# Differential score products over 64 rows each, in alternate halves of the array

## The chip, the cores and the metric

The kernel runs on one core of one Trainium2 chip. The metric is the time of one execution in microseconds of device time, the median of several runs; smaller is better.

## The reference

One decoder layer, in float32: 2048 positions, width 1024. A norm, a projection to queries, keys and values, two groups of attention heads beside each other, an output projection, a residual sum, and an MLP of width 4096 with a squared ReLU. The change touches the differential heads alone. There are four; each has two maps of 64 dimensions, whose softmaxes are subtracted:

```python
def diff_attn_block(q1, q2, k1, k2, v, lam, slopes, q0):
    def probs(q, k):
        s = jnp.einsum('bhqd,bhkd->bhqk', q, k).astype(jnp.float32) * scale + bias
        s = jnp.where(causal, s, -jnp.inf)
        return jax.nn.softmax(s, axis=-1)

    a = probs(q1, k1) - lam * probs(q2, k2)
    return jnp.einsum('bhqk,bhkd->bhqd', a.astype(v.dtype), v)
```

Eight stick-breaking heads of 64 dimensions stand beside them, with a product over later positions in place of the softmax.

## The kernel before

**Precision.** TensorE works on a rounded 4-byte type (`F32R`). To keep the result close to float32, each operand is split into a high part and a low part (what the rounding dropped), and a product is a sum of partial products: high by high, high by low, low by high. Dense products (`product`) have three partial products for each 128 rows of contraction.

**Scores.** A map has 64 dimensions, half of the array's 128 rows. The kernel before fills the other half with the key's low part: `load_k` puts the high part of both maps' keys into partitions 0 to 63 and the low part into 64 to 127 (dimension `t` of the scratch tensor `d_qk`, beside map `m`, row `r`, column `c`). The query must then stand in both halves, so `load_q` loads it twice, once into each; `j` chooses its high or its low part. One map's scores of 128 queries against up to 512 keys are two products over 128 rows: the high query against both parts of the key, and the low query against both. On the diagonal, columns left of `c0` are not computed, so that products of 512, 384, 256 and 128 columns occur. After the two products, VectorE adds the position bias on the way out of PSUM and takes the extreme value (`tensor_tensor_reduce`), and ScalarE takes the exponent.

**Loops.** `emit_diff` is called for each head and each block of 512 queries; in it run two groups `g` of 256 queries, over the key blocks `cc` before them, over two tiles `i2` of 128 queries, and over the two maps `m`. That gives 320 score tiles. Later steps of it weigh the maps, transpose the result on TensorE, and multiply by the values. `emit_sb` has 320 score tiles of its own.

**Order.** Nothing runs in the order in which it is written. Calls are recorded by `Plan.add` as units: on TensorE, successive products into the same tile are one unit, up to `LIMIT` (8). There are three streams, `dense` (projections, output, MLP), `diff` and `sb`. `Plan.order` then plays the program through with a duration for each unit (`Plan.duration`), and whenever an engine is free it takes the best unit that is ready and whose tiles find room. On TensorE attention units go first, and dense units fill what is left. `place` finds the room: PSUM has eight banks, and `caps` allows two of them to hold scores (`s`), of both kinds of heads together. `used` counts the banks held, `queue` keeps the tiles of one kind and stream in order. What comes out is a fixed list for each engine; on the chip an engine that waits holds up everything behind it in its list. All transfers are issued by one queue, SP's, in the planned order.

**Blocks.** The four blocks of 512 positions are worked in turn: projections of blocks 3 and 2, attention of 3 and 2 beside the projections of 1 and 0 and the first dense work after it, and so on; the MLPs of the last blocks stand alone at the end.

Of the kernel before, what the change touches and what calls it, by code (L numbers as in the profile page):

```python
# [20 lines left out]
F32R = mybir.dt.float32r  # L21
# [7 lines left out]
P = 128  # L29
# [3 lines left out]
HD = 64  # L33
HW = 256
# [72 lines left out]
class Plan:  # L107

    LIMIT = 8

    def __init__(self, homes):
        self.units, self.stream = [], "dense"
# [10 lines left out]
    def add(self, eng, fn, method, args, kw):  # L125
        views = [(k, v) for k, v in [*enumerate(args), *kw.items()] if isinstance(v, View)]
        outs = [v for k, v in views if k in ("out", "accum_out", 0)]
        ins = [v for k, v in views if k not in ("out", "accum_out", 0)]
        out = (outs or ins)[0]
        u = self.units[-1] if self.units else None  # L130
        if not (eng == "PE" and u and u.eng == "PE" and u.out is out.tile and len(u.calls) < self.LIMIT
                and u.stream == self.stream):
            u = Unit(len(self.units), eng, self.stream)
            u.out = out.tile
            self.units.append(u)
        u.calls.append((fn, args, kw))
        u.dur += self.duration(eng, method, kw, out, ins, u)
        for v in ins:
            for lo, hi, w in v.tile.writes:
                if lo < v.cols[1] and hi > v.cols[0]:  # L140
                    u.deps.add(w)
            v.tile.reads.append((*v.cols, u))
        for v in outs:
            for lst in (v.tile.writes, v.tile.reads):
                for lo, hi, w in lst:
                    if lo < v.cols[1] and hi > v.cols[0]:
                        u.deps.add(w)
                lst[:] = [x for x in lst if not (v.cols[0] <= x[0] and x[1] <= v.cols[1]) or x[2] is u and lst is v.tile.reads]
            v.tile.writes.append((*v.cols, u))
        if eng == "PE":  # L150

            u.deps.update(w for w in out.tile.units if w.eng == "PE")
        u.deps.discard(u)
        for v in outs + ins:
            if not v.tile.units or v.tile.units[-1] is not u:
                v.tile.units.append(u)
            if v.tile.home is not None and v.tile.units[0] is not u:
                u.deps.add(v.tile.units[0])

    def duration(self, eng, method, kw, out, ins, u):  # L160
        n = math.prod(out.shape[1:])
        small = [v for v in ins if math.prod(v.shape[1:]) * 4 > n]
        sb = [v for v in small if v.tile.home != "psum"]
        if eng == "PE":
            if kw.get("lhsT", kw.get("in_")).dtype == F32:
                return 0.112
            return max(0.058, n * 0.000442 + 0.001)
        if eng == "DVE":
            u.dual = len(sb) > 1
            u.psum = any(v.tile.home == "psum" for v in ins)  # L170
            if method == "tensor_tensor_scan":
                return 0.15 + n * 0.0022
            if method == "tensor_reduce":
                n = math.prod(ins[0].shape[1:])
            if method == "tensor_copy" and sb and n >= 256:
                u.dual = True
                return 0.43
            extra = 0.055 if isinstance(kw.get("scalar"), View) else 0.085 if "accum_out" in kw else 0.0
            return 0.15 + n / 960 + extra
        if eng == "ACT":  # L180
            u.psum = any(v.tile.home == "psum" for v in ins)
            extra = 0.09 if isinstance(kw.get("scale"), View) or isinstance(kw.get("bias"), View) else 0.0
            return 0.18 + (0.0 if u.psum else 0.03) + n / 1200 + extra + (0.19 if "accum_out" in kw else 0.0)
        if eng == "POOL":
            if method == "memset":
                return 0.2 + n / 1000
            if kw.get("op") == ALU.pow:
                return 1.65
            u.dual = True
            if method == "tensor_tensor":  # L190
                return 0.19 + n * (0.00216 if out.dtype == F32R else 0.00165)
            if method == "affine_select":
                return 0.3
            return 0.19 + n * 0.00085
        row = min([out.shape[-1]] + [v.shape[-1] for v in ins])
        u.bytes = math.prod(out.shape) * 4
        u.moves = u.bytes / {P: 265e3, HW: 300e3, BW: 335e3, D: 360e3}.get(row, 200e3)
        return 0.06


    def order(self, slots, phase_of, caps, log=None):
# [28 lines left out]
        queue = {}  # L230
# [19 lines left out]
        used = {}  # L250
# [44 lines left out]
        done, out = 0, []  # L295
# [7 lines left out]
        while done < len(units):  # L303
# [14 lines left out]
            while progress:  # L318
                progress = False
                for e in avail:  # L320
# [3 lines left out]
                    for u in waiting[e]:  # L324
                        if u.ready > now + 1e-9:
                            continue
                        k = self.key(u, now)
                        if best is not None and k >= best[0]:
                            continue
                        if u.stream == "dense" and u.i > dense[at_dense].i + self.AHEAD:  # L330
                            continue
                        spots, ok = [], True
                        for t in u.allocs:
                            if queue[u.stream, self.line(t)][-1] is not t:
                                ok = False
                                break
                            s = place(t, now)
                            if s is None:
                                ok = False
                                break  # L340
                            spots.append((t, s))
                            if len(u.allocs) > 1:
                                free[s[0]].remove(s[1])
                        if len(u.allocs) > 1:
                            for t, s in spots:
                                free[s[0]].append(s[1])
                        if ok:
                            best = k, u, spots
                    if best is None:
# [2 lines left out]
                    _, u, spots = best  # L352
# [9 lines left out]
                    start = now  # L362
                    if u.dual:
                        start = max(now, lock["POOL" if e == "DVE" else "DVE"])
# [33 lines left out]
                    for t in users.get(id(u), ()):  # L398
# [7 lines left out]
                        if not t.left:  # L406
                            kind, name = t.slot
# [43 lines left out]
def layer_kernel(ctx: ExitStack, tc: tile.TileContext, a: dict, out: bass.AP):  # L451
# [13 lines left out]
    plan = Plan(homes)  # L465
# [9 lines left out]
    def att(tag, shape, dtype=F32):  # L475
        return tile_view(tag, shape, dtype, tag)

    def dma(out, in_):

        f = [x.bitcast(F32) if x.dtype == F32R else x for x in (out, in_)]  # L480
        sp.dma_start(out=f[0], in_=f[1])

    def ps(tag):
        return tile_view("psum", [P, BW], F32, tag)
# [250 lines left out]
    def emit_diff(h, b):  # L735
        nch = NB - b

        def load_q(g):

            src = d_qk["dq", h, b][:, :, :, g * HW:(g + 1) * HW].rearrange("m t r c -> r m t c")  # L740
            qa = att("qa", [P, 2, 2, HW], F32R)
            for i in range(2):
                dma(qa[i * HD:(i + 1) * HD], src)
            return qa

        def load_k(c):
            ka = att("ka", [P, 2, BW], F32R)
            dma(ka, d_qk["dk", h, c].rearrange("m t r c -> (t r) m c"))
            return ka

        def load_v(c, kp):
# [5 lines left out]
        for g in range(NQ // 2):  # L757
# [3 lines left out]
            qa = load_q(g)  # L761
            for cc in range(nch):
                ka = load_k(b + cc)
                for i2 in range(2):
                    i = 2 * g + i2
                    c0 = i * P if cc == 0 else 0
                    for m in range(2):
                        s = ps("s")
                        qs = slice(i2 * P, (i2 + 1) * P)
                        for j in range(2):  # L770
                            pe.matmul(out=s[:, c0:], lhsT=qa[:, m, j, qs], rhs=ka[:, m, c0:], start=j == 0, stop=j == 1)

                        nm = negm[:, i2, m, cc:cc + 1]
                        t = att("e", [P, BW])
                        vec.tensor_tensor_reduce(out=t[:, c0:], in0=s[:, c0:], in1=bias[:, cc == 0, 0:BW - c0],
                                                 scale=-SLOPES[h], scalar=3e38, op0=ALU.add, op1=ALU.min, accum_out=nm)
                        act.activation(out=t[:, c0:], in_=t[:, c0:], func=ACTF.Exp, scale=-1.0, bias=nm,
                                       accum_out=l[:, i2, m, cc:cc + 1])
                        e[cc, i2, m] = t
                        yield  # L780
# [22 lines left out]
            for cc in range(nch):  # L803
                for i2 in range(2):
                    c0 = (2 * g + i2) * P if cc == 0 else 0
# [382 lines left out]
```

## Time and profile before

| | us |
|---|---|
| median of 3 runs (lowest, highest) | 2986.47 (2984.6, 2993.63) |
| the profiled execution | 2983.26 |
| its span, first to last instruction | 2981.5 |

The views used below are: the profile page (busy time of each engine and its share of the span); busy time by stretches; waits by engine; the chain of work that ended last; groups of instructions of one operation and shape (busy time, mean length of one, idle time of the engine just before them); and the timeline, in which neighbours of one kind are merged into one line with a count. All instructions go through one helper, so all have the line L446, and groups are told apart by tiles: `s<-ka,qa` are differential scores, `s<-ska,sq` those of the stick-breaking heads, `d` and `dn` dense products, `pt` transposes. PE is TensorE, PEld its weight loads, SPq the queue that issues transfers. Ends of matmuls in the trace are modelled, their starts are not.

### The profile page before, as it was taken

How to read it: one execution, taken by the hardware profiler on the slowest of the kernel's cores; microseconds unless marked ns; L12 is line 12 of the kernel's file. 1: busy time of each engine (PE TensorE's matmuls, PEld its weight loads, DVE VectorE, ACT ScalarE, POOL GpSimd, SP SyncE). 2: the span in 40 equal slices, each digit the busy share in tenths (PEclk: the TensorE clock that was granted, in tenths of full speed). 3: DMA queues.
4: the chain of work that ended last, by engine and by line, in shares of the span. 5: the costliest groups of instructions: out<-in, count | busy, mean ns of one | idle time of the engine just before them, and what ended most of it. 6: DMA issues, size and time to landing. Idle time of an engine off the chain costs nothing. (4 is left out here: it accounts for less than half of the span.)

```text
span 2981.5 us, 42384 instructions
## 1 busy us (share of the span) xinstructions
PE 2897.2 (97%) x14928; PEld 2438.1 (82%) x14928; DVE 1776.1 (60%) x3193; ACT 1146.2 (38%) x2390; POOL 1096.3 (37%) x1589
## 2 busy tenths in 40 slices
PE   8999999999999999999999999999999999999997
PEld 6889889888877887888788888888888888888886
DVE  5243477777788878786687788888543333421112
ACT  4232245555555655554354555555220110211001
POOL 3221266544776876866444344444100000000000
PEclk9999999999999999999999999999999999999998
DMA  7776988766976777877856565555874556635551
GB/s 260 254 239 204 280 255 256 216 219 210 312 247 228 249 257 241 268 255 266 313 197 204 186 198 190 189 190 172 315 270 176 205 174 243 253 132 214 204 190 65
DMA packets 304164, 670.51 MB, mean 225 GB/s; under 512 B 26960, under 2 KB 121424, under 8 KB 303952
## 3 DMA queue, kind: packets, MB, share of 16 engines
q1 hardware_dynamic: 303952, 667.80, 66.5%
q8 instruction: 119, 1.95, 0.3%
q14 instruction: 93, 0.76, 0.1%
HBM read 491.53 MB, written 176.16 MB: 224 GB/s over the span
## 5 line engine op out<-in xcount | busy, mean ns | idle before, releaser
L446 PE MATMUL d<-b,w 128*128 128x512 f32 x5376 | 1297.9, 395 | 15.0 <-ACT b L446 12.2
L446 PEld LDWEIGHTS d<-b,w 128*128 128x128 f32 x5376 | 1004.8, 189 | 233.5 <-ACT b L446 12.6
L446 PE MATMUL dn<-y,w 128*128 128x512 f32 x3072 | 748.5, 395 | 1.4 <-DVE b L446 1.1
L446 PEld LDWEIGHTS dn<-y,w 128*128 128x128 f32 x3072 | 573.2, 188 | 129.1 <-DVE b L446 1.3
L446 DVE TENSOR_TENSOR b<-b,dn 128x512 f32<-128x512 f32 x416 | 284.1, 684 | 300.9 <-PE dn L446 297.2
L446 POOL TENSOR_TENSOR w<-x,w 128x256 fp32r<-128x256 f32 x384 | 327.4, 874 | 256.3 <-ACT w L446 203.8
L446 POOL TENSOR_TENSOR set<-ser 128x512 f32<-128x512 f32 (+3 forms) x320 | 315.1, 987 | 114.8 <-DVE ser L446 100.2
L446 POOL TENSOR_TENSOR rrx<-rvx,mhalf 128x4 f32<-128x4 f32 x12 | 12.1, 1008 | 861.1 <-DVE rvx L446 861.1
L446 ACT ACTIVATE d<-d 128x512 f32<-128x512 f32 x128 | 74.8, 585 | 604.9 <-DVE d L446 604.6
L446 DVE TENSOR_TENSOR_SCAN ser<-set,left 128x512 f32<-128x512 f32 x192 | 274.7, 1435 | 9.6 <-POOL set L446 6.9
L446 DVE SCALAR_TENSOR_TENSOR d<-d,b 128x512 f32<-128x512 f32 x128 | 89.0, 698 | 303.1 <-PE d L446 294.3
L446 ACT ACTIVATE e<-e,negm 128x512 f32<-128x512 f32 (+3 forms) x320 | 209.9, 656 | 130.9 <-DVE negm L446 127.0
L446 ACT ACTIVATE hb<-pt 128x512 fp32r<-128x512 f32 (+1 forms) x320 | 164.4, 532 | 184.3 <-PE pt L446 108.6
L446 POOL TENSOR_SCALAR set<-set 128x512 f32<-128x512 f32 (+1 forms) x160 | 111.7, 698 | 315.9 <-ACT set L446 311.5
L446 DVE TENSOR_TENSOR hb<-pt,hb 128x512 fp32r<-128x512 f32 (+1 forms) x320 | 187.6, 602 | 48.5 <-ACT hb L446 46.7
L446 ACT ACTIVATE set<-s 128x512 f32<-128x512 f32 (+1 forms) x320 | 165.2, 533 | 131.1 <-PE s L446 122.3
L446 PE MATMUL d<-w,b 128*128 128x256 f32 x1536 | 201.7, 286 | 5.3 <-DMA w<-d_w_v 2.4
L446 DVE CUSTOM_DVE_ANT_0 e<-s,bias 128x512 f32<-128x512 f32 (+3 forms) x320 | 191.6, 599 | 24.8 <-PE s L446 24.5
L446 PEld LDWEIGHTS d<-w,b 128*128 128x128 f32 x1536 | 192.2, 191 | 10.8 <-DVE y L446 5.3
L446 PE MATMUL os<-hb,sv 128*128 128x512 f32 (+3 forms) x640 | 190.0, 376 | 8.1 <-DVE hb L446 2.9
L446 PE MATMUL s<-ska,sq 128*128 128x512 f32 (+3 forms) x640 | 181.4, 379 | 12.1 <-issue 3.4
L446 PE MATMUL s<-ka,qa 128*128 128x512 f32 (+3 forms) x640 | 179.1, 377 | 6.5 <-DMA qa<-d_dq 3.6
(91 smaller groups left out, 3042.0 us busy)
## 6 DMA issues: line engine op xcount, KB each, us to landing
w<-d_w_up SPq DMA_DIRECT2D x192, 512.0 KB, 5.6
w<-d_w_down SPq DMA_DIRECT2D x192, 512.0 KB, 5.0
ka<-d_dk SPq DMA_DIRECT2D x80, 512.0 KB, 5.3
v<-d_dv SPq DMA_DIRECT2D x144, 256.0 KB, 3.8
d_w_up<-w SPq DMA_DIRECT2D x64, 512.0 KB, 6.2
d_w_down<-w SPq DMA_DIRECT2D x64, 512.0 KB, 6.2
w<-d_w_out SPq DMA_DIRECT2D x48, 512.0 KB, 8.0
ska<-d_sk SPq DMA_DIRECT2D x80, 256.0 KB, 4.1
```

The lines of the kernel that those rows point to most:

```text
L446: fn(*[v.ap() if isinstance(v, View) else v for v in args], **{k: v.ap() if isinstance(v, View) else v for k, v in kw.items()})
```

## The change

Each half of the array now works on a map of its own. `load_q` puts map 0 of the query, high and low part, into partitions 0 to 63 and map 1 into 64 to 127, once; `load_k` puts the keys of map 0 into the lower half and those of map 1 into the upper, high and low part beside each other, in two transfers. The scores of both maps are allocated together, in two banks, and computed by six products over 64 rows each, which alternate between the maps: high by high, high by low, low by high. The partial product of the two low parts, which the kernel before had computed, is left out.

The planner learns three things. `joined` makes the six products one unit, although they write two tiles. A product with 64 rows in its stationary operand is costed at 0.55 of one of 128. And when a unit allocates more than one tile, the trial placement now also moves the queue and the count of held banks on, and puts them back, so that two tiles of one kind can be placed together.

```diff
-    LIMIT = 8
+    LIMIT, joined = 8, None
...
-        if not (eng == "PE" and u and u.eng == "PE" and u.out is out.tile and len(u.calls) < self.LIMIT
-                and u.stream == self.stream):
+        if eng == "PE" and self.joined and self.joined is u:
+            pass
+        elif not (eng == "PE" and u and u.eng == "PE" and u.out is out.tile and len(u.calls) < self.LIMIT
+                  and u.stream == self.stream and not self.joined):
             u = Unit(len(self.units), eng, self.stream)
             u.out = out.tile
             self.units.append(u)
+            if self.joined is True:
+                self.joined = u
...
-            return max(0.058, n * 0.000442 + 0.001)
+            return max(0.058, n * 0.000442 + 0.001) * (0.55 if kw["lhsT"].shape[0] == HD else 1.0)
...
                             if len(u.allocs) > 1:
                                 free[s[0]].remove(s[1])
+                                queue[u.stream, self.line(t)].pop()
+                                name = t.name if t.home == "psum" else (t.home, s[0])
+                                used[name] = used.get(name, 0) + 1
                         if len(u.allocs) > 1:
-                            for t, s in spots:
+                            for t, s in reversed(spots):
                                 free[s[0]].append(s[1])
+                                queue[u.stream, self.line(t)].append(t)
+                                used[t.name if t.home == "psum" else (t.home, s[0])] -= 1
...
         def load_q(g):
 
-            src = d_qk["dq", h, b][:, :, :, g * HW:(g + 1) * HW].rearrange("m t r c -> r m t c")
-            qa = att("qa", [P, 2, 2, HW], F32R)
-            for i in range(2):
-                dma(qa[i * HD:(i + 1) * HD], src)
+            qa = att("qa", [P, 2, HW], F32R)
+            src = d_qk["dq", h, b][:, :, :, g * HW:(g + 1) * HW]
+            for m in range(2):
+                dma(qa[m * HD:(m + 1) * HD], src[m].rearrange("t r c -> r t c"))
             return qa
 
         def load_k(c):
             ka = att("ka", [P, 2, BW], F32R)
-            dma(ka, d_qk["dk", h, c].rearrange("m t r c -> (t r) m c"))
+            for m in range(2):
+                dma(ka[m * HD:(m + 1) * HD], d_qk["dk", h, c][m].rearrange("t r c -> r t c"))
             return ka
...
-                    for m in range(2):
-                        s = ps("s")
-                        qs = slice(i2 * P, (i2 + 1) * P)
-                        for j in range(2):
-                            pe.matmul(out=s[:, c0:], lhsT=qa[:, m, j, qs], rhs=ka[:, m, c0:], start=j == 0, stop=j == 1)
+                    qs = slice(i2 * P, (i2 + 1) * P)
+                    ss = [ps("s") for _ in range(2)]
+
+                    plan.joined = True
+                    for n, (j, t) in enumerate(((0, 0), (0, 1), (1, 0))):
+                        for m, s in enumerate(ss):
+                            r = slice(m * HD, (m + 1) * HD)
+                            pe.matmul(out=s[:, c0:], lhsT=qa[r, j, qs], rhs=ka[r, t, c0:], start=n == 0, stop=n == 2)
+                    plan.joined = None
+                    for m, s in enumerate(ss):
```

## Rows read from the trace of the kernel before

**Rows 1.** The profile page: busy us, share of the span, number of instructions.
```profile
PE 2897.2 (97%) x14928; PEld 2438.1 (82%) x14928; DVE 1776.1 (60%) x3193; ACT 1146.2 (38%) x2390; POOL 1096.3 (37%) x1589
```

**Rows 2.** Busy time by stretch, PE, PEld, DVE, ACT, POOL; PEclk; DMA.
```profile
330.00:2070.00 1740.00, 1688.76 (x9255) 1437.39 (x9254) 1344.10 (x2559) 915.30 (x2018) 986.82 (x1455) 1.00 0.72 233
2110.00:2970.00 860.00, 855.22 (x3741) 698.42 (x3740) 276.54 (x406) 113.45 (x176) 10.18 (x10) 1.00 0.56 204
```

**Rows 3.** Waits of TensorE: us in total, times, longest us.
```profile
PE d L446 <- ACT b L446: 12.2, 2, 7.2
...
PE s L446 <- DMA qa<-d_dq: 3.6, 5, 1.3
```

**Rows 4.** The chain that ended last, in the MLP: start us, us, what.
```profile
2274.09 11.12 PE dn L446 x48
2285.21 11.00 PE d L446 x48
```

**Rows 5.** Score groups: busy us, mean ns | idle before, releaser (page, then by shape).
```profile
L446 PE MATMUL s<-ska,sq 128*128 128x512 f32 (+3 forms) x640 | 181.4, 379 | 12.1 <-issue 3.4
L446 PE MATMUL s<-ka,qa 128*128 128x512 f32 (+3 forms) x640 | 179.1, 377 | 6.5 <-DMA qa<-d_dq 3.6
...
L446 PE MATMUL s<-ka,qa 128*128 128x512 f32 x448 | 141.1, 408 | 3.9 <-DMA qa<-d_dq 2.5 <-DVE negm L446 0.9 <-ACT y L446 0.5
L446 PE MATMUL s<-ka,qa 128*128 128x384 f32 x64 | 16.4, 347 | 0.3 <-ACT set L446 0.3
L446 PE MATMUL s<-ka,qa 128*128 128x256 f32 x64 | 11.8, 294 | 2.3 <-DMA qa<-d_dq 1.1 <-ACT ha L446 0.5 <-ACT set L446 0.3
L446 PE MATMUL s<-ka,qa 128*128 128x128 f32 x64 | 11.6, 272 | 0.0
```

**Rows 6.** Timeline of TensorE, four score runs, each with what follows it.
```profile
1066.86 0.62 PE L446 MATMUL s<-ka,qa 128*128 128x512 f32 x2
1067.32 2.97 PE L446 MATMUL dn<-y,w 128*128 128x512 f32 x12
...
449.61 0.51 PE L446 MATMUL s<-ka,qa 128*128 128x384 f32 x2
449.96 0.51 PE L446 MATMUL s<-ska,sq 128*128 128x384 f32 x2
...
386.21 0.63 PE L446 MATMUL s<-ka,qa 128*128 128x256 f32 x4
386.68 1.99 PE L446 MATMUL d<-b,w 128*128 128x512 f32 x8
...
354.12 0.56 PE L446 MATMUL s<-ka,qa 128*128 128x128 f32 x4
354.51 0.90 PE L446 MATMUL d<-b,w 128*128 128x512 f32 x3
```

**Rows 7.** Timeline of TensorE: transposes between dense products.
```profile
1050.88 1.47 PE L446 MATMUL pt<-ident,set 128*128 128x128 f32 x12
1052.11 2.10 PE L446 MATMUL d<-b,w 128*128 128x512 f32 x8
1054.05 0.60 PE L446 MATMUL pt<-ident,set 128*128 128x128 f32 x4
1054.40 0.48 PE L446 MATMUL d<-b,w 128*128 128x512 f32 x1
```

**Rows 8.** Query and key transfers: ns to issue, min/median/max; first and last start.
```profile
L446 SPq DMA_DIRECT2D qa<-d_dq x64: 579/580/1653, 311.8 to 1972.1; - x64
...
L446 SPq DMA_DIRECT2D ka<-d_dk x80: 359/426/1353, 314.2 to 2029.7; - x80
```

**Rows 9.** Evictions of score tiles, by shape; VectorE's waits for them.
```profile
L446 DVE CUSTOM_DVE_ANT_0 e<-s,bias 128x512 f32<-128x512 f32 x224 | 152.1, 679 | 16.9 <-PE s L446 16.7
...
L446 ACT ACTIVATE set<-s 128x512 f32<-128x512 f32 x224 | 130.4, 597 | 107.5 <-PE s L446 99.4 <-PE os L446 5.1 <-POOL e L446 1.3
...
DVE e L446 <- PE s L446: 24.5, 34, 2.8
```

**Rows 10.** The longest wait of the transfer queue.
```profile
SPq L446 <- PE dn L446: 362.7, 99, 16.7
```

## The prediction

> **What bounds the kernel now.** I read the busy shares first. TensorE is busy for 97% of the span, VectorE for 60%, and every other engine for less [rows 1]. Weight loads are busy for 82%, but on the same engine and beside the products. Busy matmul time counts pipelined ends twice, so the next view is the busy time by stage. In the attention stage (330 to 2070 us, where all the score products lie) TensorE works 1688.8 of 1740 us, which leaves about 51 us idle; behind it, from 2110 us on, the MLP alone keeps it busy for 855 of 860 us, at a granted clock of 1.00, the 2.4 GHz level [rows 2]. The longest waits of TensorE are 12.2 us in all on one producer, and 3.6 us on the query load [rows 3]. So the order of work puts dense products into almost every gap of attention, and the dense work outlasts attention by some 900 us. That is the reason why I count TensorE time that the change saves or adds as time at the end, one for one: all that lies behind it in TensorE's list moves up.
>
> Durations of single matmuls mislead here. A 512-column product of the MLP has a recorded length near 400 ns, yet 48 of them take 11.12 or 11.00 us, 0.23 us each [rows 4]. I therefore price by starts: the start of a run of products, the start of what follows, and the count between. A 512-column score product takes (1067.32 - 1066.86)/2 = 0.23 us, one of 384 columns (449.96 - 449.61)/2 = 0.175, one of 256 (386.68 - 386.21)/4 = 0.118, one of 128 (354.51 - 354.12)/4 = 0.098 [rows 6]. The last two steps show a floor: from 256 to 128 columns the price falls by a sixth only. I read 0.098 us as the price of a weight load that its product is too short to cover.
>
> **The products.** The 640 differential score products are 448 of 512 columns and 64 each of 384, 256 and 128 [rows 5], four for each pair of maps: 112 pairs at 512 columns and 16 at each other width. Before: 112 x 0.92 + 16 x (0.70 + 0.47 + 0.39) = 103.0 + 25.0 = 128.0 us of TensorE. The change takes one of the four partial sums away, the one of the two low parts, and cuts the products in two: six products of 64 rows in place of four of 128. A product's price goes by its columns, so six in a row would cost more; the gain hangs on two products in the two halves of the array running side by side. No row shows a 64-row product: every form in the trace has 128 rows. The bounds:
> - side by side, weight loads side by side too: three slots for four, 0.75 x 128.0 = 96.0 us, a gain of 32.0;
> - side by side, weight loads one after another at 0.098 us: 512 columns 3 x 0.23 = 0.69 us (six loads are 0.59 and stay covered), the narrow ones 6 x 0.098 = 0.59 us each, so 112 x 0.69 + 48 x 0.59 = 77.3 + 28.3 = 105.6 us, a gain of 22.4;
> - one after another: 1.5 x 128.0 = 192.0 us, a loss of 64.0.
> I take the middle one, because the 128-column row shows weight loads setting the pace [rows 6]. That the halves do work side by side no row of this kernel shows.
>
> The Trainium skill (TensorE: Matmul & The Clock Gate, Part 3: Packing small matmuls) says that products in different row groups run at the same time, starting about 4 ns apart, and gives 3.07 times the speed for four of 32 rows. By it the sum is the first or second line above. No run here shows it yet.
>
> **Going into and out of the 64-row form.** The six products are one block (the planner may not split it), so there are 160 blocks and 320 changes between full-height products and half-height ones. No row shows such a change. The nearest one that the trace has is between f32 transposes and products: four transposes and eight products take 1054.40 - 1052.11 = 2.29 us, where eight products at 0.23 and four transposes at 0.1025 (twelve in 1.23 us) would be 2.25, so 0.04 us for two changes, 0.02 each [rows 7]. The other end is that TensorE runs empty at each change: a 512-column score product is recorded for 408 ns and hands over after 230, so its tail is 178 ns [rows 5, 6]. The range is 0 to 320 x 0.178 = 57.0 us; a negative cost is left out, since nothing is skipped at a change. I take 0.02, 6.4 us, because it is the one change of mode that the trace shows.
>
> **Sum:** -22.4 + 6.4 = -16.0 us against the profiled execution (2983.3 us, of which the span is 2981.5). The median of the runs is 3.2 us above it and I put the same difference on it: 2986.5 - 16.0 = 2970.5 us.
>
> **Two banks at once.** Before, a map's scores took one of the two score banks, were evicted, and the next map followed. Now a block starts only when both are free, and stick-breaking scores use the same two. One eviction of 512 columns is 0.68 us on VectorE and 0.60 us on ScalarE [rows 9]; a block of 0.69 us and two evictions hold a bank for about 2 us, 160 times in 1740 us, a fifth of the time. The price is nothing while the planner has dense work to put there, which it has for some 900 us beyond. With that cover gone, TensorE would sit idle before scores: now 6.5 + 12.1 = 18.6 us for both kinds together [rows 5], and if that doubled it would cost 18.6. The first eviction of a pair waits longer, as its sum ends with the fifth product instead of the second; VectorE waited 24.5 us in 34 waits for scores so far and is idle for 40% of the span [rows 1, 9], so I count nothing.
>
> **Loads.** Queries are 64 transfers of 256 KB, each issued in 0.58 us; they become 64 of half the size. Keys are 80 of 512 KB at 0.43 us of issue and become 160 of half the size [rows 8]. On the issuing queue the second key transfer stands ahead of the value loads and dense weights that follow; at the old issue time it adds at most 80 x 0.43 = 34 us over 1740, against what the smaller query transfers give back. The queue has slack: it waits 362.7 us for free MLP buffers alone [rows 10]. Uncovered, a key would come 0.43 us later; TensorE's whole waiting on queries is 3.6 us and keys stand nowhere in that view [rows 3]. I count nothing. HBM traffic falls by 32 x 256 KB, 8.4 MB of 670.
>
> **The planner.** It costs the block at 0.55 of a full-height product each and so plans a new order for everything behind. Its count of banks inside a trial placement is mended, which matters for units that take two tiles of one kind, and only the new blocks do. A new order moves TensorE's 51 us of attention idle about; I allow 9 us either way, about a sixth of it, and no sign.
>
> **The rivals.**
> 1. *The changes of mode cost the whole tail.* Then -22.4 + 57.0 = +34.6, 3021 us: slower. It decides from 22.4/320 = 0.07 us for each change. For it: the next block's weights may have to wait for the array to empty. Against: the transposes' 0.02 us. The Trainium skill (TensorEngine Tiling (Array Packing), section Key Properties) says that changing the tiling mode, not only the tile, drains the engine; by its drain at the trace's tail the sum is this rival's, and the transposes, which are full height, cannot refute it.
> 2. *The halves don't run side by side* (the change doesn't do what it says, for this 4-byte type): +64.0 and 6.4 for changes, 3057 us. It decides from 0.67 of a full price for each 64-row product.
> 3. *The saving goes into waits*: scores that wait for two banks, +18.6 on -16.0, +2.6, so 2989 us, no difference. For it: the score groups have idle time already. Against: little of it, 6.5 us, is before differential scores.
>
> **How the numbers follow.** The forecast 0.52, rival 1 0.20, rival 2 0.13, rival 3 0.15. The forecast's own range is 2946 to 2984: the better bound of the products with no cost of changes and 9 us of order (-32.0 - 9), and on the other side some 14 us of part of rival 3 or dearer changes. The whole range runs to 3026, rival 1 with some of the order's allowance; it leaves out rival 2 and little else. A measurement tells 0.3%, 9 us. Faster by that: most of the forecast and none of the rest, 0.46; within it: the rest of the forecast and rival 3, 0.22; slower: rivals 1 and 2, 0.32.
>
> **What would show it.** In the trace of the changed kernel, the two products of a slot should start within a few tens of ns, and a 512-column block should take about 0.70 us from its first product to the next full-height one. A block of 1.4 us is rival 2. Starts in pairs with a gap of about 0.18 us ahead of the block and behind it is rival 1. Idle time before score groups of more than 30 us is rival 3. The prediction is also wrong if work saved in attention doesn't bring the end forward: then TensorE's idle time between 330 and 2070 us has grown well past 51.

## The result: 3030 us, and the profile after

| | us |
|---|---|
| before, median of the runs beside it (lowest, highest) | 2987.66 (2984.6, 2993.63) |
| changed, median of 4 runs (lowest, highest) | 3030.36 (3026.06, 3034.7) |
| ratio, with its 95% interval | 1.014 (1.0119 to 1.0162) |
| span of the profiled execution after | 3032.9 |

The change costs 43 us. It was forecast to gain 16. The profiled execution is the slowest of the four (3034.7 us). The page of the changed kernel (busy us, share, instructions) against [rows 1]:

```profile
PE 2940.8 (97%) x15248; PEld 2409.4 (79%) x15248; DVE 1770.0 (58%) x3193; ACT 1144.6 (38%) x2390; POOL 1101.0 (36%) x1589
```

TensorE is busy 43.6 us longer, though three slots stand where four stood. By stretch (the columns of [rows 2]), the changed kernel:

```profile
330.00:2070.00 1740.00, 1679.19 (x9312) 1367.49 (x9311) 1305.06 (x2495) 889.66 (x1963) 979.68 (x1433) 0.98 0.71 223
2110.00:2970.00 860.00, 860.00 (x3822) 703.99 (x3821) 299.05 (x449) 124.82 (x200) 23.65 (x26) 1.00 0.59 214
```

In the attention stage TensorE is idle 61 us in place of 51, and its mean granted clock is 0.98 in place of 1.00. Now the timeline of TensorE around one block of scores, as in [rows 6]:

```profile
1050.05 1.99 PE L455 MATMUL d<-b,w 128*128 128x512 f32 x8
1051.97 0.96 PE L455 MATMUL s<-ka,qa 64*128 64x512 f32 x6
1052.86 2.12 PE L455 MATMUL d<-b,w 128*128 128x512 f32 x8
1054.82 0.39 PE L455 MATMUL os<-hb,sv 128*128 128x512 f32 x1
```

Price it by starts. The first eight products take 1.92 us, the block 0.89, the next eight 1.96: 4.77 us. At 0.23 us a slot, 8 + 3 + 8 slots are 4.37. So 0.40 us are lost around one block, 0.08 before it, 0.20 inside, 0.12 behind. The four products of before would have cost 0.92 us. The block with its edges costs 0.69 + 0.40 = 1.09.

This block is an ordinary one. In the trace 55 blocks of 512 columns stand between dense products of 512 columns. Their medians, from start to start, are 0.32 us from the last dense product to the block, 0.335, 0.231 and 0.328 for the three slots, and 0.338 for the first dense product behind. Against 0.23 us each, going in costs 0.09 before the block and 0.105 in its first slot, and coming out costs 0.10 in the last slot and 0.11 in the product behind.

Do the halves work side by side? This view counts the instructions that touch the queries in two short stretches of the same block (PE busy and count, PEld busy and count, clock, DMA):

```profile
1051.95:1052.00 0.05, 0.03 (x2) 0.04 (x2) 1.00 1.19 492
1052.00:1052.25 0.25, 0.25 (x2) 0.25 (x4) 1.00 1.00 410
```

Within the first 0.05 us two products and two weight loads have begun, and no third product comes in the next 0.25. The halves work side by side, and so do their weight loads. The narrow blocks say the same, one of 128 columns for example:

```profile
600.41 0.55 PE L455 MATMUL s<-ka,qa 64*128 64x128 f32 x6
600.89 0.73 PE L455 MATMUL d<-b,w 128*128 128x512 f32 x2
```

It takes 0.48 us with an edge inside. Six weight loads in turn at 0.098 us would need 0.59.

The queue's part shows in the transfers of keys and queries (ns to issue, min/median/max), against [rows 8]:

```profile
L455 SPq DMA_DIRECT2D ka<-d_dk x160: 573/580/1655, 312.9 to 2080.6; - x160
L455 SPq DMA_DIRECT2D qa<-d_dq x64: 573/580/1580, 310.5 to 2030.8; - x64
```

A key transfer of half the size is issued in 0.58 us, where the whole one took 0.43. And TensorE's waits on loads, against [rows 3]:

```profile
PE os L455 <- DMA sv<-d_sv: 10.4, 6, 2.9
PE s L455 <- DMA sq<-d_sq: 6.7, 4, 2.6
PE od L455 <- DMA v<-d_dv: 4.6, 5, 1.7
PE s L455 <- DMA ska<-d_sk: 3.7, 3, 2.0
...
PE s L455 <- DMA qa<-d_dq: 0.6, 1, 0.6
```

They sum to 26.0 us. In the kernel before, the same five sum to 14.4: 3.6 for `qa` [rows 3], and

```profile
PE od L446 <- DMA v<-d_dv: 6.6, 7, 2.2
PE s L446 <- DMA sq<-d_sq: 1.7, 3, 0.9
PE os L446 <- DMA sv<-d_sv: 1.6, 2, 1.1
PE s L446 <- DMA ska<-d_sk: 0.9, 1, 0.9
```

The differential queries come in time now; stick-breaking queries, keys and values come late.

### The profile page after: what moved, and what is told of

The parts are those of the page before. It is cut to its first block, busy times and chain, and to the rows that moved or that the text cites. A ratio compares the mean times of both kernels' runs of the same rounds, so it can differ in the third digit from the quotient of the medians.

```text
span 3032.9 us, 43094 instructions
## 1 busy us (share of the span) xinstructions
PE 2940.8 (97%) x15248; PEld 2409.4 (79%) x15248; DVE 1770.0 (58%) x3193; ACT 1144.6 (38%) x2390; POOL 1101.0 (36%) x1589
## 4 chain that ended last, share of the span: by engine, by line
PE 89%; DMA 4%; DVE 3%; POOL 2%; ACT 1%; issue 1%; SPq 0%; POOLq 0%; DVEq 0%; ACTq 0%
PE d L455 44%; PE dn L455 23%; PE s L455 8%; PE pt L455 6%; PE os L455 4%; PE od L455 3%; DMA sq<-d_sq 1%; DVE b L455 1%; DMA v<-d_dv 1%; POOL w L455 1%; DMA sv<-d_sv 1%; DVE e L455 1%; PE r L455 0%; DMA ska<-d_sk 0%; POOL e L455 0%
## 5 line engine op out<-in xcount | busy, mean ns | idle before, releaser
L455 PE MATMUL d<-b,w 128*128 128x512 f32 x5376 | 1312.3, 397 | 14.9 <-ACT b L455 11.9
L455 POOL TENSOR_TENSOR w<-x,w 128x256 fp32r<-128x256 f32 x384 | 336.6, 898 | 246.4 <-ACT w L455 181.8
L455 PE MATMUL pt<-ident,set 128*128 128x128 f32 x1088 | 156.8, 281 | 3.3 <-POOL set L455 3.3
```

The costliest lines, as they stand in the source:

```text
L455: fn(*[v.ap() if isinstance(v, View) else v for v in args], **{k: v.ap() if isinstance(v, View) else v for k, v in kw.items()})
```

## The experiments

The kernel before was run again beside each group of experiments; its medians there lie between 2985.9 and 2990.0 us, so steps between groups are uncertain by some 4 us. Two theories stood against each other at first: that the changes between the 64-row and the full-height form cost the time (M), or that the new order does, with its pairs of banks (O). The first four kernels were to tell them apart.

**Three full-height products in place of six of 64 rows, in the changed kernel's order.**

```diff
-                    for n, (j, t) in enumerate(((0, 0), (0, 1), (1, 0))):
...
+                    for s, j, t, a_, z_ in ((ss[0], 0, 0, True, False), (ss[1], 1, 0, True, True), (ss[0], 0, 1, False, True)):
+                        pe.matmul(out=s[:, c0:], lhsT=qa[:, j, qs], rhs=ka[:, t, c0:], start=a_, stop=z_)
```

> The six 64-row products of a block become three full-height ones, planned at the block's old price, so that the order of every engine is the changed kernel's; the scores are then sums over both maps, which the result is not. Theory M (changes of mode cost): the trace of the changed kernel has, for each block, about 0.09 us more ahead of it, 0.106 more in its first slot, 0.095 more behind its last and 0.11 more in the next product, some 0.40 us; 160 x 0.40 = 64 us go, 3030 - 64 = 2966 us. Theory O (the new order, with its pairs of banks and longer stalls, costs the time): the slots are three as before, so 3020 to 3030 us.

Measured 2994.2 us (ratio to before 1.002, 1.0009 to 1.0031). The changes of form cost 36 us here, so M holds in kind. But 2994 is 28 above the 2966 that M expected: with one slot fewer than before and no change of form it is still no faster than before. So something else costs time too.

**Twice as many changes of form.** The middle slot of each block is one full-height product.

```diff
                     for n, (j, t) in enumerate(((0, 0), (0, 1), (1, 0))):
+                        if n == 1:
+                            pe.matmul(out=ss[0][:, c0:], lhsT=qa[:, j, qs], rhs=ka[:, t, c0:], start=False, stop=False)
+                            continue
```

> The middle slot of each block becomes one full-height product (the scores are then wrong sums), the first and the last stay pairs of 64-row products: still three slots, the same order of all engines, but four changes between the forms in each block in place of two. Theory M: another 160 x 0.40 = 64 us, 3094 us. Theory O: no difference from 3030, within 10 us.

Measured 3083.0 us, 53 more than the changed kernel, where M expected 64. With 0, 320 and 640 changes, in the same order of every engine, the time is 2994, 3030, 3083: M again, and O's "no difference" is out for this part.

**The same products, not alternating.**

```diff
-                    for n, (j, t) in enumerate(((0, 0), (0, 1), (1, 0))):
-                        for m, s in enumerate(ss):
+                    for m, s in enumerate(ss):
+                        for n, (j, t) in enumerate(((0, 0), (0, 1), (1, 0))):
```

> The same six products of 64 rows in the same planned order of units, but map 0's three first and then map 1's three, so that neighbours are in the same half. If the halves work side by side: three more slots a block, 112 x 0.69 + 16 x (0.52 + 0.35 + 0.25) = 95 us more, 3125 us. If they work one after another in the changed kernel too: 3030 us.

Measured 3032.7 us, as the changed kernel. By the time alone the halves would not overlap. The trace says otherwise. The same count as above, at the start of one of its blocks:

```profile
1049.86:1049.91 0.05, 0.04 (x2) 0.04 (x2) 1.00 0.41 164
1049.91:1050.17 0.26, 0.26 (x2) 0.26 (x4) 1.00 1.01 410
```

Two products begin at once again, although the list has three for one half and then three for the other. The view does not name the halves, but the waits in the trace tell them apart: only the first product of a map has something to wait for (its keys, its bank), and in 133 of the 160 blocks it is the first two weight loads to start that wait for a signal (139 in the changed kernel). So the first product of the second half starts ahead of the second product of the first. The expectation was wrong in its premise: the list's order inside a block of six does not set which products overlap, and the alternation that the change writes out is not needed.

**Paired blocks with the operands, transfers and four products of before.**

```diff
+                    for j in range(2):
+                        for m, s in enumerate(ss):
+                            pe.matmul(out=s[:, c0:], lhsT=qa[:, m, j, qs], rhs=ka[:, m, c0:], start=j == 0, stop=j == 1)
```

> The changed planner and the pair of banks for each block, but the operands, transfers and four full-height products of the kernel before, alternating between the banks. Theory M: four full-height products cost what they cost before, so 2988 us, within 10. Theory O: two thirds or more of the loss stay, 3015 to 3030 us.

Measured 3007.7 us (1.0053 to 1.0088 times before): between the two theories. Is it the luck of one order? Three nudges of the planner asked that.

> The kernel before, with one thing else: the planner takes a product's time as 0.444 ns a column in place of 0.442, which reshuffles the order of every engine without any reason in the chip. If the order of the kernel before is an ordinary one: 2988 us, within 10. If it is a good one among its like, and any new order loses what it had: 2998 to 3015 us.

> The same question with another nudge: the planner's margin is 0.41 us in place of 0.40, which changes the order less. Ordinary order before: 2988 us, within 10. A good one among its like: 2995 to 3015 us.

> The changed kernel with the planner's 0.444 in place of 0.442. If the changed kernel's order is an unlucky one among its like: 3005 to 3020 us. If its loss beyond the changes of mode comes with what the change does to any order: 3025 to 3040 us.

They gave 2993.2, 2987.3 and 3030.5 us. New orders of the kernel before stay within 6.4 us of the median beside them, and another order of the changed kernel is as slow as the first. Luck of the order is out as the main cause. The same held when the planner was told the true price of a block:

> The changed kernel with the planner told the price that the trace shows for a block with its edges: half a product's time and 0.067 us for each 64-row product, so 1.08 us for a block of 512 columns in place of 0.75. If the planner's too low price makes the stalls: 3005 to 3015 us. If not: 3030 us, within what a new order does, 10.

It gave 3031.2 us: the too low price in the planner costs nothing that can be measured.

**Single transfers.** What was left of the change were its loads, which the prediction had counted as nothing. Here each is one transfer; the query loads, left out below, change likewise, and so does the layout in which both are written to scratch.

```diff
-    d_qk = {(nm, e, b): dt(f"d_{nm}{e}_{b}", [2, 2, HD, BW]) for nm in ("dq", "dk", "sq", "sk")
+    d_qk = {(nm, e, b): dt(f"d_{nm}{e}_{b}", [2, HD, 2, BW] if nm[0] == "d" else [2, 2, HD, BW]) for nm in ("dq", "dk", "sq", "sk")
...
-            for m in range(2):
-                dma(ka[m * HD:(m + 1) * HD], d_qk["dk", h, c][m].rearrange("t r c -> r t c"))
+            dma(ka, d_qk["dk", h, c].rearrange("m r t c -> (m r) t c"))
```

> The changed kernel with its keys and queries laid out in scratch so that each load is one transfer over all 128 partitions (80 key and 32 query transfers in place of 160 and 64). In the trace of the changed kernel a key transfer still takes 0.58 us to issue at half the size, 160 x 0.58 = 93 us of the queue where 80 x 0.43 = 34 stood before, and TensorE waits more for value and stick-breaking loads. If these transfers hold up the loads behind them: 3010 to 3018 us. If not: 3025 to 3035 us.

Measured 2994.8 us, 35.6 less than the changed kernel and more than was expected. This is the cause that was missing: new orders moved a kernel by 6.4 us at most, and a turned layout alone gave nothing that can be told (below, "Cheaper issue"). The key transfers of the new kernel, and its TensorE waits on loads:

```profile
L455 SPq DMA_DIRECT2D ka<-d_dk x80: 319/368/1201, 313.0 to 2046.3; - x80
...
PE s L455 <- DMA ska<-d_sk: 6.6, 4, 2.7
...
PE s L455 <- DMA sq<-d_sq: 2.6, 2, 2.3
PE os L455 <- DMA sv<-d_sv: 2.4, 3, 0.9
PE od L455 <- DMA v<-d_dv: 2.2, 3, 1.8
```

The waits are 13.8 us in place of 26.0, and the granted clock of the attention stage is 1.00 again in the profiled execution, the fastest of ten (2987.45 us):

```profile
330.00:2070.00 1740.00, 1704.94 (x9552) 1393.53 (x9550) 1329.52 (x2544) 910.84 (x2002) 978.17 (x1455) 1.00 0.69 228
```

**More room for scores, and longer blocks.** Three kernels tried to save the 64-row form: three score banks in place of two, two pairs in one block of four banks, and the latter with single transfers.

```diff
-        return dict(s=2, pt=3, od=1, os=1, r=1)[kind]
+        return dict(s=3, pt=2, od=1, os=1, r=1)[kind]
```

> The changed kernel with three banks for scores and two for transposes in place of two and three, so that a pair need not wait for both banks and a stick-breaking score can stand beside a pair. If the pair of banks costs what the kernel with paired full-height products showed (18 us): 3005 to 3018 us. If the third transpose bank is worth more: 3030 to 3050 us.

> Two pairs in one block: 12 products of 64 rows in four banks (transposes get two), so that there are 160 changes between the forms in place of 320. The step from three full-height products to the changed kernel was 36 us for 320 changes, the next one 53, so half of 320 is 18 to 27 us: 3003 to 3012 us, if four score banks cost no more than two did; 3020 to 3040 us, if the smaller room for other banks takes it back.

> Two pairs in a block and the loads as single transfers together. If both are worth what is hoped and add up: 2985 to 3000 us, level with the kernel before. If room in PSUM takes it back: 3010 to 3030 us.

They gave 3050.7, 3060.7 and 3027.2 us. Each took one bank from the transposes, and each was slower than its like with three (3030, 3030, 2995). Halving the changes doesn't pay here for the room it needs.

**The transfers alone, in the kernel before.**

```diff
-            dma(ka, d_qk["dk", h, c].rearrange("m t r c -> (t r) m c"))
+            for t in range(2):
+                dma(ka[t * HD:(t + 1) * HD], d_qk["dk", h, c][:, t].rearrange("m r c -> r m c"))
```

> The kernel before with one part of the change alone: each key load in two transfers of half the partitions, 160 of 256 KB in place of 80 of 512 KB; products as before. If the transfers were the larger part of the loss: 3010 to 3025 us. If they cost only beside paired blocks: 2985 to 2995 us.

Measured 3005.0 us (1.003 to 1.007 times before): 17 us from this line alone, more than a new order moved this kernel (6.4 us) and half of the 35.6 that the split of keys and queries costs in the changed kernel. Its two longest waits of TensorE on loads:

```profile
PE s L446 <- DMA qa<-d_dq: 14.6, 9, 5.6
PE od L446 <- DMA v<-d_dv: 14.0, 15, 3.3
```

With `sv`, `ska` and `sq` (4.2, 3.8 and 2.0) the loads of attention are waited for 38.6 us, where 14.4 stood before.

**Three and four full-height products with single transfers**, in one order.

> Single transfers, and three full-height products in place of the six of 64 rows, in the same order (the scores are then sums over both maps). Against the kernel with single transfers and 64-row products (2995 us) the step is the price of 320 changes of form with the transfers out of the way. At the 48 us by which TensorE's time at the blocks differed: 2947 us. At 36 as in the pair of runs with double transfers: 2959 us. If the changes hide: 2985 to 2995 us.

> Single transfers and paired blocks of four full-height products (sums over both maps, so not the scores), in the same order as the three of the kernel at 2942 us. A fourth product is 112 x 0.23 + 16 x (0.175 + 0.118 + 0.098) = 32 us: 2974 us. If that holds, the pair of banks costs nothing beside the kernel before (2987), and smaller transfers give 13 back; 2985 us or more would mean that stalls grow with TensorE's work.

They gave 2942.3 and 2970.9 us. So a slot in each pair is worth 28.6 us (worked out: 32), and the 320 changes of form cost 2994.8 - 2942.3 = 52.5 us when loads hold TensorE up less. The split of the loads costs 2994.2 - 2942.3 = 51.9 us in the full-height form, against 35.6 in the 64-row form: the two costs do not simply add. In [rows 5] the score groups wait for `qa` and others; with three full-height products and single transfers the widest has no idle time left:

```profile
L455 PE MATMUL s<-ka,qa 128*128 128x512 f32 x336 | 97.9, 399 | 0.0
```

**Cheaper issue.** If the queue is what binds, cheaper loads should help the kernel before as well, in its unchanged order, and the changed one further.

> The kernel before with the order of every engine unchanged and its products unchanged; only the scratch layout of queries, keys and stick-breaking queries is turned so that what goes to one partition lies together, which should shorten the issue of these loads (0.58 and 0.43 us each before). If the queue's issue time holds TensorE up also there: 2970 to 2980 us, better than both kernels. If only the doubled transfers mattered: 2986 us, within 5.

> The changed kernel with single transfers for keys and queries, and the stick-breaking queries laid out together as well. If the queue's issue time is still felt: 2980 to 2990 us. If the queue has slack again: 2995 us, within 5.

Measured 2983.8 us (0.9972 to 1.0001 times before) and 2994.6. The first is no difference that can be told from the kernel before, the second none from the 2994.8 us above. The issue of a query transfer fell only to 0.54 us and of a stick-breaking query to 0.46, so little was saved, and the two say only that this little is not felt.

**Paired blocks again.**

> Paired blocks of four full-height products with the operands and transfers of the kernel before, under another order (0.444 in place of 0.442 in the planner). If the 18 us of the first such kernel are the luck of its order: 2985 to 2998 us. If the pair of banks costs them: 3003 to 3012 us.

Measured 3001.1 us (1.0018 to 1.005 times before). Paired blocks with the transfers of before are 11 and 18 us slower than the kernel before beside them, under two orders; with single transfers and undoubled queries (2970.9) they are 19 faster. Pairing, the loads and the smaller queries do not simply add. What part of those 30 us is the number of query transfers, what their size, and what the key layout, no run separates.

## Why the prediction was wrong, step by step

**The bound** was right in kind: TensorE's time passes to the end, though not one for one. A slot less gave 28.6 us of 32.0, and the changes of form took 52.5 us, or 36 where loads hold TensorE up, of some 60. The reading of the waits left out two of the longest: between the lines of [rows 3] stand 9.4 us on a producer and 6.6 on the value load, the longest wait on a load.

**The products** were right in the mechanism. The halves run side by side. The choice between the two bounds (22.4 and 32.0) was the wrong one: the weight loads of the two halves begin together as well. The bounds differ in the narrow blocks alone, and there the pairs start 0.112 us apart at 128 columns (median of six blocks between dense products), where two loads in turn would need 0.196. The 28.6 us were measured on full-height products and do not decide this.

**Going into and out of the form** is the first step that failed: 0.02 us for each change was taken, 6.4 us in all. The runs give 52.5/320 = 0.164 us, close to the upper end, 0.178. The choice went by the row of transposes, because it was the only change of mode in the trace, and transposes are full height: the row was near in looks and not in kind. The upper end was priced too narrowly, too. It counted the emptying of the array and left out that the next weight load then has nothing to hide behind: at each edge the starts show some 0.10 us of a late start and then 0.11 us more before the next product can follow, about a weight load. That the second part is the load is a reading; the loads stand in the trace at that place.

So a change costs 0.20 us by the trace. At 0.40 us a block that is 64 us in all; summed over all 160 blocks and their neighbours, the two kernels with single transfers differ by 60, those with split ones by 48. The time shows 52.5 and 36. Part of the gap is waits that shrink when TensorE comes later: with split transfers, the waits on the five loads are 36.9, 26.0 and 19.7 us at 0, 320 and 640 changes. Another part may be the clock: the kernel with three full-height products and split transfers ran at a mean granted clock of 0.987 (median of ten executions), the changed one at 0.991; 0.004 of 2994 us is about 12 us. The Trainium skill (TensorEngine Tiling (Array Packing), section Key Properties) says that a change of tiling mode drains the engine; the trace agrees, with 0.09 us before the first 64-row product and 0.10 behind the last.

**The loads** are the second step that failed, and the one that no rival named. They were counted at nothing because the queue has long waits. Two errors: the issue time was carried over from the whole transfer (0.43 us), while a half transfer over 64 partitions took 0.58, as the query transfers of that shape already did in [rows 8]; so the queue gives 160 x 0.58 = 93 us to keys, not 160 x 0.43 = 69. And long waits of the queue for free buffers at some moments are no reserve at others: the loads of the other heads stand behind the keys in the one queue, and TensorE's waits for the loads of attention rose from 14.4 us to 38.6 when the keys alone were split. Single transfers gave 35.6 us back. Whether it is the issue time, the number of transfers or another property of the halves that delays the loads, no run separates. The Trainium skill (DMA: Bandwidth & Descriptors, section Rules for kernel authors) advises one transfer over 128 partitions in place of two to halves; the runs agree (17 us in the kernel before for the keys, 36 in the changed one for keys and queries), with the issue time as the visible cost.

**Two banks, and the planner.** The planner's price cost nothing, as said. Pairing was counted at nothing; it cost 11 to 18 us with the transfers of before, and no cost can be seen beside single ones.

The parts by the medians, from the kernel before: paired blocks with single, undoubled loads -17, the fourth slot -29, the changes of form +52, the split of the transfers +36, together +42, where +43 was measured. These are steps of one chain of kernels, so they add up by construction; as the two costs do not simply add, another path would share them out otherwise.

Of the rivals the first, "the whole tail at each change", had the right mechanism and about the right size for its part, 57.0 against 52.5; its sign, a gap of 0.18 us ahead of the block and behind it, came as 0.09 and 0.10 with as much again in the product that follows. Its total, 3021, missed for the loads. Of the other signs, pairs do start within a few ns, a block takes 0.89 us in place of 0.70, and the idle time in attention grew to 61 us, not well past 51.

How late loads turn into more than their own wait: 26.0 against 13.8 us of waits, each from one execution, are a third of the 35.6. A stretch of the changed kernel shows one more way (idle time in brackets):

```profile
1067.27 1.56 PE L455 MATMUL dn<-y,w 128*128 128x512 f32 x6
1070.84 2.04 PE L455 MATMUL s<-ska,sq 128*128 128x512 f32 x6 [2.00 <-DMA ska<-d_sk]
1072.68 1.05 PE L455 MATMUL os<-hb,sv 128*128 128x512 f32 x2
1073.53 1.05 PE L455 MATMUL s<-ska,sq 128*128 128x512 f32 x2
```

and the granted clock around it (the third value from the end of a line, before DMA share and GB/s):

```profile
1067.00:1068.80 1.80, 1.80 (x8) 1.12 (x6) 0.81 (x3) 0.00 (x0) 0.20 (x2) 1.00 1.07 337
1072.00:1075.20 3.20, 3.20 (x9) 2.47 (x8) 0.00 (x0) 2.98 (x7) 2.22 (x5) 0.50 0.75 256
1076.00:1080.00 4.00, 4.00 (x22) 2.95 (x21) 3.49 (x8) 2.72 (x6) 2.27 (x6) 1.00 0.83 272
```

Behind an idle time of 2.00 us for a stick-breaking key load the clock stands at 0.50, the 1.2 GHz level, and two products take (1073.53 - 1072.68)/2 = 0.43 us each in place of 0.23. But this is a small part of the 35.6 us. The 0.98 of the attention stage belongs to one execution, whose mean clock over the whole span is 0.987; the three others of the changed kernel have 0.991 or 0.992 and still take 3026 to 3031 us, and those with single transfers have 0.991 to 0.993. A thousandth of the span is 3 us. So most of what the late loads cost beyond their own waits stays open.

## What to carry to other kernels

Here a block of half-height products gains one slot of 0.23 us for each three and pays 0.16 us at each of its two edges, so blocks of six such products between full-height work lose. By these numbers a block has to save two slots to gain; that is an estimate, and the one kernel here whose blocks save two (3027 us with single transfers) lost more by the banks that it took. Price each transfer by its own shape, not by that of the one it replaces, and do not take a queue that waits often for a queue with slack: look at what stands behind the transfer. And when a bound is chosen by the nearest row, ask whether that row shares the mechanism, not only the name.

## What was not expected of the hardware

Products of 64 rows ran in pairs also when the list had all three of one half ahead of those of the other (3032.7 against 3030.4 us): their starts are 10 ns apart then, and 3 to 4 ns when they alternate (medians of 160 blocks). And a key transfer of 256 KB over 64 partitions took longer to issue, 0.58 us, than one of 512 KB over 128, 0.37 to 0.43, or one of 256 KB over 128 (`ska<-d_sk`), 0.42 in the same kernel.
